# The second norm of a hybrid decoder block: sums by token quarters, stored and fetched rows turned at another place

## The chip, the cores and the metric

The kernel runs on one core of a Trainium2 chip. The metric is the device time of one execution in microseconds. A profile of one execution gives the span (first to last instruction), each instruction's start and duration, and what each engine waited for. The engines are PE (TensorE, with PEld its weight loads), DVE (VectorE), ACT (ScalarE), POOL (GpSimd) and SP, whose queue starts most transfers.

## The reference, cut to what matters

```python
x = x + gate1[:, None, :] * (merged @ w_out[l])
h2 = modulate(rmsnorm(x, norm2_g[l]), shift2, scale2)
x = x + gate2[:, None, :] * peer(h2, peer_wq[l], peer_subkeys[l], peer_u[l], peer_v[l])
# rmsnorm: x * rsqrt(mean(x*x, -1) + EPS) * g;   modulate: h * (1 + scale) + shift
# peer: q = h2 @ wq, 16 blocks of 128 columns (8 heads, 2 halves); scores of each half with 128
# subkeys; the best 16 of each half, then the best 16 of the sums: 128 experts for a token, each
# a row of peer_u and of peer_v, weighted by softmax(scores) * gelu(u . h2)
```

There are 512 tokens and 1024 channels, all in float32. Ahead of this lie the first norm, the input projection, attention and a short convolution; the change leaves them alone.

## The kernel before, in words

Activations lie transposed: `xT` holds 8 blocks of 128 channels by 512 tokens. A float32 product is made from three products of float32r parts (`hi`, made on ScalarE, and `lo` = value minus `hi`, made on VectorE or GpSimd in `split`), by `mm3`: 3 matmuls for each block of 128 channels, 24 for a whole block of outputs. Instructions are issued by a framework that lays out each engine's queue from the dependencies and its own estimate of times: code order is a priority, and an instruction whose inputs are ready may go ahead of earlier code. `after(ins, mark)` adds a wait by hand. `mark[0]` is the last matmul of the latest `mm3`. Tiles of one tag share a fixed number of buffers; the pools `xp` (`xT`) and `tp` (temporary tiles) are closed after the second norm and their space is used again by `r4` and `rp` (subkeys `sk`, queries `qs`, scores).

The path around the change:

- *Output product* (`out_half`, loop at L540): for each of 8 blocks, 24 matmuls into a bank `py`, then VectorE updates `xT` with the gate (L544). ScalarE squares the block before it and VectorE adds the squares up (`squared`, L219). Beside it `more_ada` computes the modulation columns `mod` 30 to 47, three blocks in each of six rounds (L213).
- *Second norm*: the sum of squares over channels is a product with `ones` in a bank `ss2` (L551 for blocks 0 to 6, L552 for block 7), which gives every partition the sums of all 512 tokens. `rstd` (L239) takes root and reciprocal on 128 x 512. The columns `s2` = (1 + scale) * gain are made by L553 and L554 after it in the code.
- `spill` (L528): 32 transposes of `xT` (each 128 x 128), 8 copies `xn` to SBUF and 8 stores to `x1s` in DRAM, so that the rows of x can be added at the kernel's end. They wait for `end`, the last matmul of the sum.
- *Early query blocks*: for two query blocks (`EARLY`) the weights are split ahead, by VectorE. For each of 8 channel blocks `modulated` makes `f` on VectorE (L229), `fH` on ScalarE (L230), `fL` on VectorE (L231), and the 6 matmuls of both query blocks follow.
- *Rows of the fetched tokens* (L584): the last 160 of the 512 tokens get their experts by fetched rows. ScalarE adds the shift to those columns of `f` (L590 spreads the 32 tokens before `TD` over 96 columns more; L592), TensorE transposes 8 blocks for each of two row tiles, ScalarE copies them to `hN` and `h2N`.
- *Query stage* (`query`, `scores`, L721 to L757): for each of 16 blocks 24 matmuls (blocks 0 and 1 have theirs), a copy `qs`, then the scores of the block before (L738: 4 float32 products, 8 instructions), and the best 16 on VectorE (`level1`, `level2`). GpSimd makes the `lo` parts of these weights. After it the dense expert stage begins (`first`).

Of the kernel before, what the change touches and what calls it, by code (L numbers as in the profile page):

```python
# [89 lines left out]
def body(tc, p):  # L90
# [83 lines left out]

    def split(h, l, f, by=nc.vector):
        nc.scalar.activation(h, f, AF.Copy)  # L176
        by.tensor_sub(l, f, h.bitcast(F32))  # L177

# [4 lines left out]

    def parts(src, by=nc.vector):

        raw = load(src)
        h = hl.tile([P, D], F32R, tag="h", bufs=4, name="hi")
        l = hl.tile([P, D], F32R, tag="l", bufs=4, name="lo")
        split(h, l, raw, by)
        return h, l  # L190

    def weights_of(src, by=nc.vector):

        h, l = parts(src.rearrange("p a b -> p (a b)"), by)
        return (lambda k: h[:, k * P:(k + 1) * P]), (lambda k: l[:, k * P:(k + 1) * P])
# [20 lines left out]
    def tmp(name):  # L216
        return tp.tile([P, T], F32, name=name, **T2)
# [16 lines left out]
    def square(ps, b, i, n, w=None):  # L234
        q = tmp("sq")
        nc.scalar.activation(q, b, AF.Square)
        nc.tensor.matmul(ps, ones if w is None else w, q, start=(i == 0), stop=(i == n - 1))

    def rstd(ps, n):  # L239
# [287 lines left out]

    def spill(half, when):  # L528
        for c in range(NCH):
            ps = bank("xt")  # L530
            for i in range(4):
                after(nc.tensor.transpose(ps[:, i * P:(i + 1) * P], xT[:, 4 * half + i, c * P:(c + 1) * P], ident),
                      when)
            xn = rt.tile([P, 512], F32, name="xn", **R2)
            nc.scalar.activation(xn, ps, AF.Copy)
            nc.sync.dma_start(x1s[c][:, half * 512:(half + 1) * 512], xn)

    ss2 = bank("ss2")
    sq = None
    for b in range(DC):  # L540
        if b >= HEAD:
            out_half(b, 0)
        out_half(b, 1)
        nc.vector.scalar_tensor_tensor(xT[:, b, :], py.pop(b), mod[:, 16 + b:17 + b], xT[:, b, :],  # L544
                                       op0=OP.mult, op1=OP.add)
        if 0 < b < DC - 1:
            sq = squared(xT[:, b - 1, :], sq)
        if b < 6:
            more_ada(3)
    sq = squared(xT[:, 6, :], sq)  # L550
    nc.tensor.matmul(ss2, ones, sq, start=True, stop=False)  # L551
    end = nc.tensor.matmul(ss2, ones, squared(xT[:, 7, :]), start=False, stop=True)  # L552
    nc.vector.tensor_add(mod[:, 24:48], mod[:, 24:48], ab[:, 24:48])  # L553
    nc.vector.scalar_tensor_tensor(s2, mod[:, 32:40], 1.0, S("n2g"), op0=OP.add, op1=OP.mult)  # L554
    a1_s.close()
# [18 lines left out]
    fL = hx.tile([P, DC, T], F32R, name="fL")  # L574
    r2 = rstd(ss2, D)
    spill(0, end)
    spill(1, end)
    early = [(weights_of(p["wq"][b]), bank("pq")) for b in range(EARLY)]
    fs = []
    for k in range(DC):  # L580
        fs.append(modulated(fH[:, k, :], fL[:, k, :], xT[:, k, :], r2, s2[:, k:k + 1], mod[:, 24 + k:25 + k]))
        for w, o in early:
            mm3(o, w, lambda k: fH[:, k, :], lambda k: fL[:, k, :], [k])
    for r, (dst, cs) in enumerate(((hN, slice(TD - P, TD)), (h2N, slice(TD, T)))):  # L584
        pg = [bank("pg0"), bank("pg1")]
        for k in range(DC):
            b = mod[:, 24 + k:25 + k]
            f = fs[k]
            if r == 0:
                nc.scalar.activation(f[:, TD - P:TU].rearrange("p (q t) -> p q t", t=HT),  # L590
                                     f[:, None, TU:TD].to_broadcast([P, P // HT - 1, HT]), AF.Identity, bias=b)
                nc.scalar.activation(f[:, TU:T], f[:, TU:T], AF.Identity, bias=b)  # L592
            nc.tensor.transpose(pg[k // 4][:, (k % 4) * P:(k % 4 + 1) * P], f[:, cs], ident)
        for k in range(2):
            nc.scalar.activation(dst[:, k * 512:(k + 1) * 512], pg[k], AF.Copy)
    xp_s.close()
# [121 lines left out]
    def tmp(name):  # L718
        return rp.tile([P, T], F32, tag="t2", name=name, bufs=4)

    def query(hp):  # L721
        sk = rp.tile([P, P], F32, tag="sk", name="sk", bufs=3)
        if hp < EARLY:
            ps = early[hp][1]
        else:
            w = weights_of(p["wq"][hp], nc.gpsimd)
            ps = bank("pq")
            mm3(ps, w, lambda k: fH[:, k, :], lambda k: fL[:, k, :])
        nc.sync.dma_start(sk, p["sk"][hp])
        qs = tmp("qs")  # L730
        nc.scalar.activation(qs, ps, AF.Copy)
        return qs, sk
# [15 lines left out]
    for hp in range(16):  # L748
        so_far = mark[0]
        now = query(hp)  # L750
        if last:
            scores(hp - 1, *last)
            if 2 <= hp < 2 + DC:
                for d, x in ((h2H, fH), (h2L, fL)):
                    after(nc.scalar.activation(d[:, hp - 2, :], x[:, hp - 2, 0:TU].bitcast(F32), AF.Copy), so_far)
        last = now
    scores(15, *last)  # L757
# [374 lines left out]
```

## Time and profile before

| what | value |
|---|---|
| device time, median of 3 executions | 1435.29 us (1432.73 to 1438.98) |
| profiled execution | 1440.74 us, span 1438.9 us |
| busy: PE, PEld | 1395.2 us (97%), 1223.1 us (85%) |
| busy: DVE, ACT, POOL | 1228.5 us (85%), 615.9 us (43%), 468.0 us (33%) |
| mean granted TensorE clock | 0.989 of full |

An engine's share of busy time is an average over stages. A matmul's record lasts from its start to a modelled end, and the next one starts before that; the pace is read from two starts. The bracket behind a row of a timeline is the idle time ahead of it and the instruction that ended it. A row of a timeline can hold several like instructions in a row (x32); its duration is then that of all.

### The profile page before, as it was taken

The page shows a single profiled execution, that of the slowest core. Times are in us where ns is not written, and L with a number is a line of the kernel's source. Part 1 is how long each engine was busy: PE and PEld are TensorE (multiplying, and loading weights), DVE is VectorE, ACT ScalarE, POOL GpSimd, SP SyncE. Part 2 cuts the span into 40 slices and gives each one's busy share as a digit, 9 for nine tenths or more (in the row PEclk, how much of TensorE's full clock was granted, in tenths as well). Part 3 has the DMA queues.
Part 4 walks back from the last instruction along what each step waited for, and adds up shares of the span by engine and source line. Part 5 has one row for each costly group of instructions (what it writes and reads, how often), then busy time and mean ns, then how long its engine had stood idle before and what let it go on. Part 6 is the DMA issues. An engine that isn't in the chain of part 4 may idle for free.

```text
span 1438.9 us, 21241 instructions
## 1 busy us (share of the span) xinstructions
PE 1395.2 (97%) x7696; PEld 1223.1 (85%) x7696; DVE 1228.5 (85%) x2245; ACT 615.9 (43%) x1041; POOL 468.0 (33%) x314
## 2 busy tenths in 40 slices
PE   6999998999999999999999999999999999999998
PEld 4676766888999999989888888889999998889897
DVE  6778978689989999998778898888789889898954
ACT  4524644543735555553433343333343324333431
POOL 0000001343332330043034444546545546655300
PEclk9899999999999999999999999999999999999999
DMA  8545536222497997799999999999999999999843
GB/s 283 192 160 189 191 108 229 87 86 93 127 348 268 389 363 255 251 364 394 350 346 379 391 390 384 401 362 368 351 367 396 382 364 335 381 344 389 310 144 132
DMA packets 134377, 418.81 MB, mean 291 GB/s; under 512 B 12800, under 2 KB 39552, under 8 KB 132736
## 3 DMA queue, kind: packets, MB, share of 16 engines
q1 hardware_dynamic: 92800, 266.45, 51.4%
q0 software_dynamic: 41472, 151.01, 27.5%
q8 instruction: 60, 0.98, 0.3%
q14 instruction: 45, 0.37, 0.1%
HBM read 375.77 MB, written 41.62 MB: 290 GB/s over the span
## 4 chain that ended last, share of the span: by engine, by line
PE 40%; DMA 8%; DVE 5%; issue 5%; POOL 2%; ACT 0%; DVEq 0%; POOLq 0%; ACTq 0%
PE o L998 8%; PE o L997 8%; PE o L996 8%; PE pa L202 5%; PE pa L200 5%; PE pa L201 5%; DMA row<-in_uR,eG 4%; DMA row<-in_vL,eG 3%; POOL row L776 2%; DVE lo L177 1%; DVE junk L784 1%; DMA G<-Gd 1%; DVE ga L912 1%; DVE wwl L177 0%; DVE B L946 0%
## 5 line engine op out<-in xcount | busy, mean ns | idle before, releaser
L176 ACT ACTIVATE hi<-raw 128x1024 fp32r<-128x1024 f32 x298 | 312.5, 1053 | 300.8 <-PE pa L201 92.3
L177 DVE TENSOR_TENSOR lo<-raw,hi 128x1024 fp32r<-128x1024 f32 x276 | 336.2, 1220 | 42.0 <-ACT hi L176 36.5
L200 PE MATMUL pa<-h2H,hi 128*128 128x352 f32 x1024 | 332.9, 325 | 3.1 <-ACT sp L620 3.0
L202 PE MATMUL pa<-h2H,lo 128*128 128x352 f32 x1024 | 331.9, 324 | 3.1 <-DVE lo L177 3.1
L201 PE MATMUL pa<-h2L,hi 128*128 128x352 f32 x1024 | 329.9, 322 | 0.0
L997 PE MATMUL o<-lo,wwh 128*128 128x512 f32 x768 | 299.6, 390 | 1.8 <-DVE lo L177 1.6
L996 PE MATMUL o<-hi,wwh 128*128 128x512 f32 x768 | 299.6, 390 | 0.0
L998 PE MATMUL o<-hi,wwl 128*128 128x512 f32 x768 | 299.0, 389 | 0.2 <-DVE wwl L177 0.2
L776 POOL DMA_INDIRECT row<-in_uR,eG x128 | 190.0, 1484 | 321.0 <-PE o L998 176.9
L776 POOL DMA_INDIRECT row<-in_vL,eG x128 | 177.4, 1386 | 137.9 <-PE o L998 65.3
L784 DVE SCALAR_TENSOR_TENSOR junk<-row,h2N 128x1024 bf16<-128x1024 f32 x128 | 154.2, 1223 | 58.2 <-DMA row<-in_uR,eG 58.0
L202 PEld LDWEIGHTS pa<-h2H,lo 128*128 128x128 f32 x1024 | 194.0, 189 | 5.5 <-DVE lo L177 5.4
L200 PEld LDWEIGHTS pa<-h2H,hi 128*128 128x128 f32 x1024 | 192.8, 188 | 6.0 <-ACT sp L620 3.3
L201 PEld LDWEIGHTS pa<-h2L,hi 128*128 128x128 f32 x1024 | 193.0, 189 | 2.2
L912 DVE SCALAR_TENSOR_TENSOR ga<-row,av,ga 128x1024 f32<-128x1024 f32 x127 | 163.0, 1284 | 28.3 <-DMA row<-in_vL,eG 27.2
L997 PEld LDWEIGHTS o<-lo,wwh 128*128 128x128 f32 x768 | 144.2, 188 | 31.8 <-DVE lo L177 3.7
L998 PEld LDWEIGHTS o<-hi,wwl 128*128 128x128 f32 x768 | 144.2, 188 | 30.7 <-DVE wwl L177 0.6
L996 PEld LDWEIGHTS o<-hi,wwh 128*128 128x128 f32 x768 | 144.2, 188 | 28.0 <-issue 0.2
L177 POOL TENSOR_TENSOR lo<-raw,hi 128x1024 fp32r<-128x1024 f32 x22 | 53.4, 2429 | 322.7 <-ACT hi L176 322.7
L176 ACT ACTIVATE wwh<-w 128x768 fp32r<-128x768 f32 x64 | 54.0, 844 | 162.6 <-DVE w L979 124.3
L978 ACT ACTIVATE w<-G 128x32 f32<-128x32 f32 x128 | 22.3, 221 | 198.2 <-DVE wwl L177 187.9
L776 POOL DMA_INDIRECT row<-in_uR,eH x32 | 47.0, 1470 | 105.2 <-DVE junk L784 88.5
(266 smaller groups left out, 1912.6 us busy)
## 6 DMA issues: line engine op xcount, KB each, us to landing
raw<-in_uL SPq DMA_DIRECT2D x128, 512.0 KB, 6.3
raw<-in_vL SPq DMA_DIRECT2D x128, 512.0 KB, 6.7
Gd<-st SPq DMA_DIRECT2D x12, 2048.0 KB, 10.0
G<-Gd SPq DMA_DIRECT2D x16, 1536.0 KB, 12.5
ada<-in_ada SPq DMA_DIRECT2D x32, 512.0 KB, 4.4
Ad<-sp SPq DMA_DIRECT2D x34, 352.0 KB, 6.4
sp<-Ad SPq DMA_DIRECT2D x34, 352.0 KB, 6.8
raw<-in_w_in SPq DMA_DIRECT2D x18, 512.0 KB, 5.1
```

Source lines behind the costliest of these rows:

```text
L176: nc.scalar.activation(h, f, AF.Copy)
L177: by.tensor_sub(l, f, h.bitcast(F32))
L200: nc.tensor.matmul(ps, wh(k), rh(k), start=(k == k0), stop=False)
L201: nc.tensor.matmul(ps, wh(k), rl(k), start=False, stop=False)
L202: mark[0] = nc.tensor.matmul(ps, wl(k), rh(k), start=False, stop=(k == k1))
L776: d = nc.gpsimd.indirect_dma_start(out=t, out_offset=None, in_=tab, in_offset=bass.IndirectOffsetOnAxis(ap=e, axis=0))
L784: return nc.vector.scalar_tensor_tensor(junk, t, 1.0, h, op0=OP.mult, op1=OP.mult, accum_out=a)
L912: nc.vector.scalar_tensor_tensor(ga, t, av[:, k:k + 1], ga, op0=OP.mult, op1=OP.add)
L978: nc.scalar.activation(wv[:, i, nu:], g[:, i, nu:], AF.Copy)
L996: nc.tensor.matmul(o, wh[:, cs], vh[:, hs], start=(j == 0), stop=False)
L997: nc.tensor.matmul(o, wh[:, cs], vl[:, hs], start=False, stop=False)
L998: last = nc.tensor.matmul(o, wl[:, cs], vh[:, hs], start=False, stop=(j == NJ - 1))
```

## The change

- The modulation columns 24 to 39 and `s2` are finished ahead of the output loop in the code; only columns 40 to 47 stay behind it.
- The `lo` part of early query block 1 waits for the update of `xT` block 6 (`x6`). GpSimd's `lo` part of query block 2 waits for `end`, that of block 3 for `begun`, the last matmul of the early query blocks.
- The sums of squares are made by `grouped`: the tokens of each quarter (128) are summed into 32 partitions of their own, so root and reciprocal run on 128 x 128 (`grouped_root`). `spread` then brings them back to 128 x 512 by four products with one column of the identity, into a PSUM bank, which `modulated` reads in place of an SBUF tile.
- 8 of the 32 transposes of x go behind the last output matmul, ahead of the sums; their 2 copies and stores wait for `end`. The other 24 transposes, 6 copies and stores wait for `begun`. The copies `xn` now use the pool of temporary tiles.
- The 16 activations that prepared the fetched tokens' columns are removed. In query blocks 5, 7, 9 and 11 GpSimd makes these columns as `fH` + `fL` (two additions in each, `f2`), and in blocks 13 and 14 TensorE transposes them and ScalarE copies them.

```diff
@@
-    def split(h, l, f, by=nc.vector):
+    def split(h, l, f, by=nc.vector, when=None):
         nc.scalar.activation(h, f, AF.Copy)
-        by.tensor_sub(l, f, h.bitcast(F32))
+        after(by.tensor_sub(l, f, h.bitcast(F32)), when)
...
+    def grouped(ps, q, first, last):
+
+        for c in range(NCH):
+            end = nc.tensor.matmul(ps[32 * c:32 * c + 32, 0:P], ones[:, 0:32], q[:, c * P:(c + 1) * P], start=first,
+                                   stop=last)
+        return end
+
+    def grouped_root(ps, n):
+        r = cp.tile([P, P], F32, tag="r", name="r", bufs=1)
+        nc.scalar.activation(r, ps[:, 0:P], AF.Sqrt, scale=1.0 / n, bias=eps)
+        nc.vector.reciprocal(r, r)
+        return r
+
+    def spread(r):
+
+        ps = psa.tile([P, 512], F32, tag="a", name="rr")
+        for c in range(NCH):
+            nc.tensor.matmul(ps[:, c * P:(c + 1) * P], ident[:, 32 * c:32 * c + 1].to_broadcast([P, P]), r,
+                             start=True, stop=True)
+        return ps
@@
-    def spill(half, when):
-        for c in range(NCH):
+    def turned(half, when, cs):
+
+        out = []
+        for c in cs:
             ps = bank("xt")
             for i in range(4):
                 after(nc.tensor.transpose(ps[:, i * P:(i + 1) * P], xT[:, 4 * half + i, c * P:(c + 1) * P], ident),
                       when)
-            xn = rt.tile([P, 512], F32, name="xn", **R2)
-            nc.scalar.activation(xn, ps, AF.Copy)
+            out.append((half, c, ps))
+        return out
+
+    def stored(blocks, when):
+        for half, c, ps in blocks:
+            xn = tmp("xn")
+            after(nc.scalar.activation(xn, ps, AF.Copy), when)
             nc.sync.dma_start(x1s[c][:, half * 512:(half + 1) * 512], xn)
 
+    nc.vector.tensor_add(mod[:, 24:40], mod[:, 24:40], ab[:, 24:40])
+    nc.vector.scalar_tensor_tensor(s2, mod[:, 32:40], 1.0, S("n2g"), op0=OP.add, op1=OP.mult)
...
+        if b == DC - 2:
+            x6 = x
...
+    some = turned(0, mark[0], range(2))
     sq = squared(xT[:, 6, :], sq)
-    nc.tensor.matmul(ss2, ones, sq, start=True, stop=False)
-    end = nc.tensor.matmul(ss2, ones, squared(xT[:, 7, :]), start=False, stop=True)
-    nc.vector.tensor_add(mod[:, 24:48], mod[:, 24:48], ab[:, 24:48])
-    nc.vector.scalar_tensor_tensor(s2, mod[:, 32:40], 1.0, S("n2g"), op0=OP.add, op1=OP.mult)
+    grouped(ss2, sq, True, False)
+    end = grouped(ss2, squared(xT[:, 7, :]), False, True)
+    nc.vector.tensor_add(mod[:, 40:48], mod[:, 40:48], ab[:, 40:48])
@@
-    r2 = rstd(ss2, D)
-    spill(0, end)
-    spill(1, end)
-    early = [(weights_of(p["wq"][b]), bank("pq")) for b in range(EARLY)]
-    fs = []
+    r2 = spread(grouped_root(ss2, D))
+    stored(some, end)
+    early = [(weights_of(p["wq"][b], when=x6 if b else None), bank("pq")) for b in range(EARLY)]
     for k in range(DC):
-        fs.append(modulated(fH[:, k, :], fL[:, k, :], xT[:, k, :], r2, s2[:, k:k + 1], mod[:, 24 + k:25 + k]))
+        modulated(fH[:, k, :], fL[:, k, :], xT[:, k, :], r2, s2[:, k:k + 1], mod[:, 24 + k:25 + k])
...
+    begun = mark[0]
+    for half, cs in ((0, range(2, NCH)), (1, range(NCH))):
+        stored(turned(half, begun, cs), begun)
@@
+    f2 = hx.tile([P, DC, 2 * P], F32, name="f2")
+
+    def rows_turned(r):
+
+        pg = [bank("pg0"), bank("pg1")]
+        for k in range(DC):
+            nc.tensor.transpose(pg[k // 4][:, (k % 4) * P:(k % 4 + 1) * P], f2[:, k, r * P:(r + 1) * P], ident)
+        for k in range(2):
+            nc.scalar.activation((hN, h2N)[r][:, k * 512:(k + 1) * 512], pg[k], AF.Copy)
...
-            w = weights_of(p["wq"][hp], nc.gpsimd)
+            w = weights_of(p["wq"][hp], nc.gpsimd, {2: end, 3: begun}.get(hp))
...
+            if hp in (5, 7, 9, 11):
+                k = slice(hp - 5, hp - 3)
+                sq = [P, 2, P // HT, HT]
+                after(nc.gpsimd.tensor_add(f2[:, k, 0:P].rearrange("p k (q t) -> p k q t", t=HT),
+                                           fH[:, k, None, TU:TD].bitcast(F32).to_broadcast(sq),
+                                           fL[:, k, None, TU:TD].bitcast(F32).to_broadcast(sq)), so_far)
+                nc.gpsimd.tensor_add(f2[:, k, P:], fH[:, k, TD:].bitcast(F32), fL[:, k, TD:].bitcast(F32))
+            if hp in (13, 14):
+                rows_turned(hp - 13)
```

## Rows read from the trace of the kernel before

**Rows 1.** Stage windows: length; PE, PEld, DVE, ACT, POOL busy; clock, DMA, GB/s

```profile
300.00:352.00 52.00, 52.00 (x265) 44.00 (x263) 46.99 (x304) 19.07 (x37) 19.25 (x8) 1.00 0.28 91
352.00:400.00 48.00, 45.76 (x288) 44.99 (x287) 46.26 (x135) 32.22 (x38) 17.64 (x9) 1.00 0.45 142
...
500.00:700.00 200.00, 192.37 (x1527) 185.32 (x1526) 192.70 (x439) 103.84 (x177) 37.94 (x25) 0.99 0.87 326
```

**Rows 2.** TensorE in order of time: start, duration, instruction, [idle before, releaser]

```profile
236.39 0.39 PE L202 MATMUL py<-mH,lo 128*128 128x512 f32 x1
238.23 1.13 PE L551 MATMUL ss<-sq,ones 128*128 128x512 f32 x2 [1.46 <-DVE sq L223]
239.56 1.12 PE L552 MATMUL ss<-sq,ones 128*128 128x512 f32 x2 [0.20 <-ACT sq L221]
240.52 3.66 PE L532 MATMUL xt<-cst,xT 128*128 128x128 f32 x32
247.16 1.22 PE L200 MATMUL pq<-fH,hi 128*128 128x512 f32 x2 [2.99 <-ACT fH L230]
...
259.38 0.39 PE L201 MATMUL pq<-fL,hi 128*128 128x512 f32 x1
259.61 0.40 PE L202 MATMUL pq<-fH,lo 128*128 128x512 f32 x1
...
261.59 1.06 PE L738 MATMUL psc<-sk,qs 128*128 128x128 f32 x8
262.40 0.48 PE L200 MATMUL pq<-fH,hi 128*128 128x512 f32 x1
```

**Rows 3.** Engines by stretch as in 1, around the clock's fall

```profile
244.20:247.10 2.90, 0.00 (x0) 0.00 (x0) 2.67 (x4) 1.80 (x4) 0.00 (x0) 1.00 0.67 256
247.10:249.00 1.90, 1.84 (x4) 1.40 (x5) 1.86 (x3) 1.90 (x5) 0.00 (x0) 0.52 0.81 312
```

**Rows 4.** VectorE in order of time, around the second norm

```profile
232.63 2.37 DVE L554 SCALAR_TENSOR_TENSOR s<-mod,sm 128x8 f32<-128x8 f32 x1
...
236.05 0.74 DVE L544 SCALAR_TENSOR_TENSOR xT<-py,mod,xT 128x512 f32<-128x512 f32 x1
237.48 0.69 DVE L223 TENSOR_TENSOR sq<-sq 128x512 f32<-128x512 f32 x1 [0.70 <-ACT sq L221]
238.09 0.75 DVE L544 SCALAR_TENSOR_TENSOR xT<-py,mod,xT 128x512 f32<-128x512 f32 x1
...
241.44 3.35 DVE L242 RECIPROCAL rstd<-rstd 128x512 f32<-128x512 f32 x1 [2.45 <-ACT rstd L241]
...
253.88 0.75 DVE L229 SCALAR_TENSOR_TENSOR f<-xT,s,rstd 128x512 f32<-128x512 f32 x1
```

**Rows 5.** ScalarE in order of time, around the second norm

```profile
238.87 0.63 ACT L221 ACTIVATE sq<-xT 128x512 f32<-128x512 f32 x1 [0.47 <-DVE xT L544]
240.72 0.69 ACT L241 ACTIVATE rstd<-ss,eps 128x512 f32<-128x512 f32 x1 [1.22 <-PE ss L552]
...
245.29 1.21 ACT L535 ACTIVATE xn<-xt 128x512 f32<-128x512 f32 x2 [2.42 <-DMA x1s<-xn]
246.39 0.71 ACT L230 ACTIVATE fH<-f,mod 128x512 fp32r<-128x512 f32 x1
```

**Rows 6.** GpSimd in order of time, before the second norm

```profile
232.34 2.62 POOL L177 TENSOR_TENSOR lo<-raw,hi 128x1024 fp32r<-128x1024 f32 x1 [231.89 <-ACT hi L176]
```

**Rows 7.** Groups by line and shape: busy, mean ns, idle before

```profile
L741 ACT ACTIVATE scg<-psc 128x128 f32<-128x128 f32 x16 | 4.5, 282 | 0.0
...
L403 DVE RECIPROCAL den<-den 128x8 f32<-128x8 f32 x4 | 0.8, 198 | 0.0
```

**Rows 8.** SP's DMA issues in order of time

```profile
254.69 1.28 SPq L729 DMA_DIRECT2D sk<-in_sk  x3
```

**Rows 9.** DMA issues by tile: size, median us to landing

```profile
sk<-in_sk SPq DMA_DIRECT2D x16, 64.0 KB, 1.7
```

More of the change, by code (lines that the diff above doesn't have):

```diff
@@ L182, in load, with parts @@
         return raw
-    def parts(src, by=nc.vector):
+    def parts(src, by=nc.vector, when=None):
         raw = load(src)
@@ L188, in parts, with weights_of @@
         l = hl.tile([P, D], F32R, tag="l", bufs=4, name="lo")
-        split(h, l, raw, by)
+        split(h, l, raw, by, when)
         return h, l
-    def weights_of(src, by=nc.vector):
-        h, l = parts(src.rearrange("p a b -> p (a b)"), by)
+    def weights_of(src, by=nc.vector, when=None):
+        h, l = parts(src.rearrange("p a b -> p (a b)"), by, when)
         return (lambda k: h[:, k * P:(k + 1) * P]), (lambda k: l[:, k * P:(k + 1) * P])
@@ L543, in body @@
         out_half(b, 1)
-        nc.vector.scalar_tensor_tensor(xT[:, b, :], py.pop(b), mod[:, 16 + b:17 + b], xT[:, b, :],
-                                       op0=OP.mult, op1=OP.add)
+        x = nc.vector.scalar_tensor_tensor(xT[:, b, :], py.pop(b), mod[:, 16 + b:17 + b], xT[:, b, :],
+                                           op0=OP.mult, op1=OP.add)
+        if b == DC - 2:
+            x6 = x
         if 0 < b < DC - 1:
@@ L574, in body @@
     fL = hx.tile([P, DC, T], F32R, name="fL")
-    r2 = rstd(ss2, D)
-    spill(0, end)
-    spill(1, end)
-    early = [(weights_of(p["wq"][b]), bank("pq")) for b in range(EARLY)]
-    fs = []
+    r2 = spread(grouped_root(ss2, D))
+    stored(some, end)
+    early = [(weights_of(p["wq"][b], when=x6 if b else None), bank("pq")) for b in range(EARLY)]
     for k in range(DC):
-        fs.append(modulated(fH[:, k, :], fL[:, k, :], xT[:, k, :], r2, s2[:, k:k + 1], mod[:, 24 + k:25 + k]))
+        modulated(fH[:, k, :], fL[:, k, :], xT[:, k, :], r2, s2[:, k:k + 1], mod[:, 24 + k:25 + k])
         for w, o in early:
             mm3(o, w, lambda k: fH[:, k, :], lambda k: fL[:, k, :], [k])
[L584 to L595, printed above, removed]
+    begun = mark[0]
+    for half, cs in ((0, range(2, NCH)), (1, range(NCH))):
+        stored(turned(half, begun, cs), begun)
     xp_s.close()
```

## The prediction, made before the result was known

> **What bounds the kernel now.** I read the stage table first. From the first query product to the end TensorE sets the pace: in the query stage it is busy in every microsecond of 300 to 352, VectorE in 46.99 of 52 [rows 1]. A microsecond that TensorE loses before 262 us is therefore a microsecond of the end, and so is each matmul added later. Next I read TensorE in order of time around the second norm [rows 2]. The last output product starts at 236.39 and lasts 0.39, so it ends at 236.78; the third query block starts at 262.40. Everything the change touches lies in these 25.6 us. TensorE idles 1.46 before the first sum of squares, about 0.2 before the second, then runs 32 transposes from 240.52, idles 2.99, and starts the query products at 247.16. [...] One such matmul follows another after 0.23 (259.38 to 259.61), so 48 want 10.9; the stretch from 247.16 to 259.84, where the next work started, was 12.7. The slow clock cost 1.7.
>
> Last I read the chain behind those gaps on VectorE, ScalarE and GpSimd [rows 4 to 6]. x of block 6 was ready to be made once its product was done (231.4, 24 matmuls before 236.78), but started at 236.05: the 8-column s2 in front of it took 2.37, for it lies inside a GpSimd lo part running from 232.34 to 234.96, and then came a lo part of VectorE's own. Block 7 then stood behind block 6's square and its addition and started at 238.09, 1.25 after the product it needs. From there: square 0.63, sum 1.12 to 240.68, root 0.69, reciprocal 3.35 on 512 columns, first scaled block at about 244.8, and its fH at 246.39 instead of about 245.6, because two copies of transposed rows, themselves held 2.42 by a store, stood ahead on ScalarE.
>
> **The change, along that path.** All times are those of the profiled execution, 1440.74 us with a span of 1438.9; the median of the runs shown is 1435.29, and I take the same difference off it.
>
> The scale s2 moves ahead, the lo part of query block 1 waits for x of block 6, and GpSimd's lo parts for blocks 2 and 3 wait for the end of the sum and of the early products. Then block 6 is done by about 232.2 and its square and addition by about 234, and block 7 starts 0.06 after its product: 236.84 to 237.59, square to 238.25. What queues behind the held parts can bear it: on VectorE only the addition and block 7; on GpSimd only later lo parts. Block 2's lo runs 2.6 from about 239.5 and is wanted near 258; block 3's runs from about 254.6 to 257.2 and is wanted 6.4 later than that of block 2.
>
> TensorE fills the wait with 8 of the 32 transposes at 0.11 each (32 took 3.66), to 237.65. The sums by quarters are new. The nearest rows are the score products, 8 instructions on 128 columns: 1.06 from start to end, 0.81 until the next work starts. Bounds: 0.27 if the four strips of 32 outputs run side by side, 1.12 if they cost what the full sum did. I take the scores' price, since shape and count are theirs: the first group to 238.46, the second to 239.5. That is 1.2 ahead of 240.68.
>
> Root on 128 columns: 0.28, as the 128-column copy from PSUM [rows 7], to 239.85. Reciprocal: 8 columns took 0.20 [rows 7] and 512 took 3.35, so 128 want 0.95, to 240.8. Spreading the quarters back over 512 columns is four more such products, 1.06, to 241.9. Then f 0.75, now read with 1/rms in PSUM (block updates, which also read PSUM, take 0.74 to 0.75 too [rows 4]), fH 0.72 with only two row copies near it, both done in the reciprocal's shadow: TensorE starts at 243.5, which is **3.6 ahead** of 247.16.
>
> Does the clock fall again? Idle 1.46 at 236.8 was not followed by a lower clock, idle 2.99 at 244.2 was [rows 2, 3]. The new gaps are about 1.35 (239.5 to 240.85) and 1.6 (241.9 to 243.5), nearest to the first. I take no fall: 48 matmuls in 10.9, to 254.5, 5.3 ahead of 259.84. VectorE keeps up, with 16 operations on eight blocks at some 0.65 each (14 of them from 244.8 to the last f at 253.88).
>
> [...]
>
> Now what was hidden comes due. The other 24 transposes stood in a wait before; now they follow the early products on a busy TensorE: 2.6, to 257.1. The 16 transposes of the fetched tokens' rows go from here to query blocks 13 and 14, where they cost the same 1.75. The scores of block 0 take 0.81, and block 2 starts at 257.9, 4.5 ahead of 262.40. With 1.75 paid later, **2.7 us** remain.
>
> Moved things that I cost at nothing: ScalarE loses 16 small activations; it is busy 19.07 of 52 in the query stage [rows 1]. The stores of x move from 242 to about 256 on SP's queue, 0.33 an issue, and are read only at the kernel's end. GpSimd gets eight additions of 256 elements; 1024 took 2.62 [rows 6], so 0.6 each, bounds 0.6 and 2.6, in blocks of 6.4 where it has one lo part of 2.6. Without that cover they would delay the lo part of a later query block. VectorE's 5 idle microseconds in 52 hide what it waits for them.
>
> **Rivals.** *The clock falls all the same.* Light work from 236.8 to 243.5 with 3 us of idling speaks for it, the short gaps against it. It costs up to 1.7: gain 1.0, 1434.3 us.
>
> *The scores wait.* The subkeys' load started at 254.69, right after the last f read xT (253.88 and 0.74) [rows 4, 8], so it seems to lie in xT's space. Now xT is read by transposes until 257.3; a load takes 1.7 to land [rows 9], so block 0's scores could start at 259.1, not 257.1. Six row copies of about 0.6 ahead of the query copy on ScalarE end near there too. If TensorE's queue has the scores ahead of block 2, 2.0 are lost: gain 0.7, 1434.6 us; with a fallen clock 1.0 slower, 1436.3. Against it: the queues are laid out by readiness, as s2, late in the code, ahead of block 6 shows.
>
> *GpSimd's additions make VectorE the bound* (the other side). The place is query blocks 5 to 12, where VectorE's candidate sums read two SBUF tensors, as s2 does. If each addition took 2.6 and held VectorE that long, 8 would give 21 against some 5 of slack: 16 late, less the 2.7, so 13 slower, 1448. It decides (7.2 slower) from 1.9 per addition on. Against it: lo parts of 2.6 in every block already lie beside a VectorE with time to spare.
>
> [...]
>
> *The rest of the program is laid out anew.* An edit here can shift orders later on. TensorE idles 2.2 from 352 to 400 and 7.6 from 500 to 700 [rows 1]; if that vanished the gain would be 12.5, 1423; if it doubled, 7.1 slower, 1442 or a little over.
>
> *The change doesn't do what it says*: block 6 stays late by another neighbour. Then 1.25 of the lead is lost, gain 1.4, 1433.9.
>
> **Numbers.** Forecast, gain 2.7: 1432.6 us, chance 0.42. Clock falls 0.22, scores wait 0.16, laid out anew 0.13, additions on GpSimd 0.04, block 6 late 0.03. The most the region could give is its idle 4.65 and the clock's 1.7, less 1.06 for spreading: 5.3, 1430.0. The worst of the small cases is 1436.3. Three runs lay from 1432.73 to 1438.98, so I widen by 1 below, and by 2 above for a milder new layout: 1429.0 to 1438.5. About 0.5%, 7.2 us, is what a measurement of this kernel tells from no change: beyond it lie, of the new layout's 0.13, 0.04 on the fast side and 0.04 on the slow one, and 0.02 of the GpSimd case. So faster 0.04, same 0.90, slower 0.06.
>
> **What would show it.** Block 6's update near 231.5 and block 7's within 0.1 of its product; a reciprocal near 0.95; the first early product near 243.5; granted clock near 1.00 in the 4 us behind it; 24 transposes back to back after the early products with no wait before the next scores; candidate sums still at 0.3. I'd be wrong if the early products start after 245, if TensorE waits for subkeys or for rows' banks near 257, or if the lead of 4.5 at block 2 does not stand at the first dense block less 1.75.

## The result and the profile after

The changed kernel takes 1446.26 us (median of 6 executions, 1442.51 to 1450.59) beside 1434.57 (6 executions, 1432.73 to 1438.98) of the kernel before: a ratio of 1.0076, 95% interval 1.0057 to 1.0096. It is 11.7 us slower where 2.7 less had been forecast, and outside the range.

| profiled execution | before | after |
|---|---|---|
| time, span | 1440.74, 1438.9 us | 1447.71, 1445.9 us |
| busy PE, DVE | 1395.2, 1228.5 us | 1392.2, 1223.5 us |
| mean granted clock | 0.989 | 0.989 |
| end of the last output product | 236.78 | 231.91 |
| first dense product | 353.7 | 359.5 |
| between these two, the *stretch* | 116.9 | 127.6 |

Nothing of this can be seen in shares of busy time. The end of the last output product varies between executions with nothing edited ahead of it (227.85 in a second profile of the kernel before), so times are best read from that point. The stretch from there to the first dense product has grown by 10.7. The rest has not: from the first dense product to the end of the span it is 1438.9 - 353.7 = 1085.2 before and 1445.9 - 359.5 = 1086.4 after (1083.3 to 1091.6 over all profiles below, 1089.2 in the second of the kernel before). Nearly all the loss lies in the stretch.

TensorE of the changed kernel in order of time, in the form of [rows 2]:

```profile
231.52 0.39 PE L202 MATMUL py<-mH,lo 128*128 128x512 f32 x1
231.75 1.04 PE L555 MATMUL xt<-cst,xT 128*128 128x128 f32 x8
232.72 0.43 PE L242 MATMUL ss<-sq,ones 128*32 128x128 f32 x8
233.42 0.43 PE L242 MATMUL ss<-sq,ones 128*32 128x128 f32 x8 [0.28 <-ACT sq L221]
235.32 1.16 PE L256 MATMUL rr<-r,cst 128*128 128x128 f32 x8 [1.47 <-DVE r L249]
238.07 1.22 PE L200 MATMUL pq<-fH,hi 128*128 128x512 f32 x2 [1.60 <-ACT fH L230]
...
252.23 2.84 PE L555 MATMUL xt<-cst,xT 128*128 128x128 f32 x24
263.27 2.04 PE L769 MATMUL psc<-sk,qs 128*128 128x128 f32 x8 [8.20 <-DMA sk<-in_sk]
264.97 0.77 PE L200 MATMUL pq<-fH,hi 128*128 128x512 f32 x1
...
272.04 1.05 PE L769 MATMUL psc<-sk,qs 128*128 128x128 f32 x8
```

The early products start 238.07 - 231.91 = 6.2 behind the last output product; before it was 247.16 - 236.78 = 10.4 [rows 2] (10.2 in the second profile of the kernel before). So the first half of the change gives 4.2. Then three things go wrong. The 48 early products last 14.16, to 252.23. The 24 transposes end at 255.07, and the scores of block 0 wait 8.20 for the subkeys. These scores and block 2 behind them are slow: 1.70 to the next start instead of 0.81, and 7.07 for the 24 products, which took 5.59 in the kernel before (262.40 to the next scores at 267.99).

The stages, as in [rows 1, 3], show the clock and the DMA:

```profile
236.50:238.00 1.50, 0.00 (x0) 0.00 (x0) 1.49 (x3) 0.70 (x2) 0.00 (x0) 0.81 0.51 184
238.00:244.00 6.00, 5.92 (x13) 4.24 (x14) 6.00 (x10) 3.37 (x6) 1.89 (x2) 0.50 0.19 73
...
254.80:263.20 8.40, 0.28 (x3) 0.04 (x1) 0.00 (x0) 3.43 (x7) 4.69 (x3) 0.69 0.90 277
259.00:266.50 7.50, 3.23 (x12) 2.97 (x13) 0.62 (x4) 0.66 (x2) 1.64 (x1) 0.50 0.96 325
...
300.00:352.00 52.00, 52.00 (x270) 44.18 (x269) 46.14 (x297) 19.93 (x41) 20.58 (x11) 1.00 0.29 91
```

The clock is 0.50 in the first six microseconds of the early products, and 0.50 again around the scores (259.00 to 266.50). While TensorE waits, the DMA engines are 0.90 busy. The query stage (last line) is as full as before.

What TensorE waits for is one line of the table of waits (engine, what, releaser: total, times, longest). SP's queue in order of time then shows why the load came so late:

```profile
PE psc L769 <- DMA sk<-in_sk: 8.2, 1, 8.2
```

```profile
234.79 0.81 SPq L564 DMA_DIRECT2D x1s<-xn  x2
236.38 18.83 SPq L181 DMA_DIRECT2D raw<-in_wq  x2
255.31 4.04 SPq L564 DMA_DIRECT2D x1s<-xn  x6
259.45 1.76 SPq L760 DMA_DIRECT2D sk<-in_sk  x3
```

The durations of the single issues of stores (ns: least, median, most):

```profile
L564 SPq DMA_DIRECT2D x1s<-xn x8: 326/413/972, 234.8 to 258.8; - x8
```

The subkeys stand behind two weight loads, the second of which holds the queue until 255.21, and behind six stores, which take 4.04. The row copies are done by 256.31 (the rows of ScalarE below), so it isn't they that make these stores slow: an issue itself lasts up to 0.97. Why is not shown. The issue of the subkeys at 259.45 is 4.4 later than the end of the last transpose, which frees the space. The scores start 3.82 after it, when the first load has landed, behind 1.5 MB of stores and half a megabyte of weights; the median landing before was 1.7 [rows 9].

VectorE, ScalarE and GpSimd, as in [rows 4 to 6]:

```profile
227.42 0.74 DVE L574 SCALAR_TENSOR_TENSOR xT<-py,mod,xT 128x512 f32<-128x512 f32 x1
...
231.95 0.75 DVE L574 SCALAR_TENSOR_TENSOR xT<-py,mod,xT 128x512 f32<-128x512 f32 x1 [1.93 <-PE py L202]
...
234.31 0.95 DVE L249 RECIPROCAL r<-r 128x128 f32<-128x128 f32 x1 [1.46 <-ACT r L248]
236.51 2.07 DVE L229 SCALAR_TENSOR_TENSOR f<-xT,s,rr 128x512 f32<-128x512 f32 x3 [1.25 <-PE rr L256]
```

```profile
233.91 0.37 ACT L248 ACTIVATE r<-ss,eps 128x128 f32<-128x128 f32 x1 [0.55 <-PE ss L242]
...
253.31 3.00 ACT L563 ACTIVATE xn<-xt 128x512 f32<-128x512 f32 x6
256.16 1.12 ACT L762 ACTIVATE qs<-pq 128x512 f32<-128x512 f32 x2
```

```profile
234.02 2.34 POOL L177 TENSOR_TENSOR lo<-raw,hi 128x1024 fp32r<-128x1024 f32 x1 [233.57 <-PE ss L242]
239.98 1.17 POOL L793 TENSOR_TENSOR f<-fH,fL 128x256 f32<-128x256 f32 x1 [3.63 <-DVE fL L231]
...
247.48 0.73 POOL L793 TENSOR_TENSOR f<-fH,fL 128x256 f32<-128x256 f32 x1 [1.65 <-DVE fL L231]
252.48 4.67 POOL L177 TENSOR_TENSOR lo<-raw,hi 128x1024 fp32r<-128x1024 f32 x2 [4.27 <-PE pq L202]
```

Block 7 starts 0.04 after its product, and the reciprocal is 0.95. The last line of GpSimd is the one that holds SP's queue: the first of these two lo parts ends near 254.8, half of 4.67 behind its start, and the second weight load, which had waited for a buffer of raw weights, is issued.

### The profile page after: what moved, and what is told of

Its sections match the earlier page's. It is cut to its first block, busy times and chain, and to the rows that moved or that the text cites. A ratio compares the mean times of both kernels' runs of the same rounds, so it can differ in the third digit from the quotient of the medians.

```text
span 1445.9 us, 21281 instructions
## 1 busy us (share of the span) xinstructions
PE 1392.2 (96%) x7716; PEld 1221.5 (84%) x7716; DVE 1223.5 (85%) x2246; ACT 611.8 (42%) x1025; POOL 459.4 (32%) x322
## 4 chain that ended last, share of the span: by engine, by line
PE 39%; issue 6%; DMA 5%; DVE 5%; POOL 3%; ACT 0%; POOLq 0%; SPq 0%; DVEq 0%
PE o L1037 7%; PE o L1038 7%; PE o L1036 7%; PE pa L200 5%; PE pa L202 5%; PE pa L201 5%; DMA row<-in_uR,eG 4%; POOL row L816 3%; DVE lo L177 1%; DVE junk L824 1%; DMA Ad<-sp 1%; DVE B L986 1%; DMA sp<-Ad 1%; DVE wwl L177 0%; DVE w L1019 0%
## 5 line engine op out<-in xcount | busy, mean ns | idle before, releaser
L816 POOL DMA_INDIRECT row<-in_uR,eG x128 | 183.7, 1435 | 331.2 <-PE o L1038 185.5
L816 POOL DMA_INDIRECT row<-in_vL,eG x128 | 168.5, 1316 | 144.1 <-PE o L1038 75.1
```

The lines of the kernel that those rows point to most:

```text
L816: d = nc.gpsimd.indirect_dma_start(out=t, out_offset=None, in_=tab, in_offset=bass.IndirectOffsetOnAxis(ap=e, axis=0))
```

## The experiments

Two theories stood at the start. *Scores* (S in the forecasts): most of the loss is block 0's scores waiting for a load that lies in `xT`'s space and queues behind stores and weights. *Holds* (H): GpSimd's held lo parts are the cause, since they hold the weight load that blocks SP. Beside both, the slow early products were to be explained. The stretch is measured in the one profiled execution of each, as in the table above. A ratio is to the kernel before as it ran beside that version, so ratios are compared and not times; their intervals reach 0.0016 to 0.0028 to either side, 2 to 4 us.

**The subkeys in a space of their own.** They need not wait for `xT`, and their load goes ahead.

```diff
-        sk = rp.tile([P, P], F32, tag="sk", name="sk", bufs=3)
+        sk = hx.tile([P, P], F32, tag="sk", name="sk", bufs=3)
```

> The changed kernel, but the subkeys' tiles lie beside fH and fL instead of in the space that xT gives back, so their first three loads stand ahead of the stores of x in SP's queue; TensorE's order is the same. Theory S (the 8.2 us wait of block 0's scores is the subkeys' load, which must wait for xT's last transposes and for six stores ahead of it in SP's queue): the wait is gone, TensorE goes from the last transposes to the scores without a gap, and the clock does not fall there, so about 8.2 of wait, 1 of slow scores and 1.4 of slow products of block 2 come back: 1435 to 1437 us. Rival H (the held lo part of block 3 blocks SP's queue by the weight load behind it): that load and the stores are where they were, so something else in the queue is still late and at most 2 us come back: 1444 or more.

Measured: 1436.70 us, ratio to before 1.0014 (0.9996 to 1.0033), stretch 118.9. This one line moves 9 of the 11.7 us. Its TensorE, then SP's queue:

```profile
237.29 1.22 PE L200 MATMUL pq<-fH,hi 128*128 128x512 f32 x2 [1.60 <-ACT fH L230]
251.43 2.84 PE L555 MATMUL xt<-cst,xT 128*128 128x128 f32 x24
256.05 1.16 PE L769 MATMUL psc<-sk,qs 128*128 128x128 f32 x8 [1.77 <-ACT qs L762]
```

```profile
231.16 1.28 SPq L760 DMA_DIRECT2D sk<-in_sk  x3
```

The wait of 8.20 is gone; what ends last now is the query copy on ScalarE, behind six row copies. The scores then take 0.91 to the next start (256.05 to 256.96), with the clock at 1.00 from 256 to 262. The early products still take 251.43 - 237.29 = 14.1. So the two losses are separate.

**No holds on GpSimd's lo parts.**

```diff
-            w = weights_of(p["wq"][hp], nc.gpsimd, {2: end, 3: begun}.get(hp))
+            w = weights_of(p["wq"][hp], nc.gpsimd, None)
```

> The changed kernel without the two holds of GpSimd's lo parts of blocks 2 and 3; SP's weight loads move ahead of the stores as a result, TensorE's order is the same. Rival H: the queue is free when the first row copy is made, the subkeys are issued near 254 in the times of the changed kernel and most of the 8.2 us wait goes: 1437 to 1440 us. Theory S: the subkeys stay behind xT's transposes and six stores; the first store leaves about 1.4 earlier (253.9 instead of 255.3) and half a megabyte less is under way, so 1 to 2.5 of the wait go: 1443 to 1445.5 us.

Measured: 1447.18 us, 1.0098 (1.0072 to 1.0124), stretch 127.9, wait 8.53. The theory of the holds falls; but the 1 to 2.5 that theory S had forecast did not go either. SP's queue and GpSimd show why:

```profile
253.10 0.33 SPq L181 DMA_DIRECT2D raw<-in_wq  x1
253.48 4.13 SPq L564 DMA_DIRECT2D x1s<-xn  x6
257.71 1.77 SPq L760 DMA_DIRECT2D sk<-in_sk  x3
```

```profile
250.71 2.36 POOL L177 TENSOR_TENSOR lo<-raw,hi 128x1024 fp32r<-128x1024 f32 x1 [4.61 <-ACT hi L176]
```

The weight load still waits for a lo part that ends at 253.07, just when the last transpose ends (253.08). That part waits for its hi part on ScalarE, which waited for the early products, whose weights hold its buffer. The hold that was taken away had another one behind it.

**The six late stores on ScalarE's queue.**

```diff
-            nc.sync.dma_start(x1s[c][:, half * 512:(half + 1) * 512], xn)
+            (nc.sync if when is end else nc.scalar).dma_start(x1s[c][:, half * 512:(half + 1) * 512], xn)
```

> The changed kernel with the six late stores of x issued from ScalarE's queue instead of SP's; the subkeys still lie in xT's space and still wait for its last transposes. It parts theory S in two. If the place behind six issues makes the wait, the subkeys are issued at about 255.3 instead of 259.45 (behind the weight load that waits for the held lo part), land in 2 to 4 us, and the wait falls from 8.2 to 2.5 to 5: 1439 to 1442 us. If it is the transfers (1.6 MB of stores at some 300 GB/s are 5 us), the subkeys land about as late as before, at 261 or later, and the wait is 6 or more: 1444 or more.

Measured: 1445.30 us, 1.0068 (1.0044 to 1.0091), stretch 127.9. It doesn't test what it was made for, since the blocking moved. SP's queue, its stores gone, took a third weight load ahead of the subkeys (issued at 258.49), and on ScalarE the query copy stood behind the issue of the stores:

```profile
257.75 6.02 ACTq L564 DMA_DIRECT2D x1s<-xn  x2
263.82 1.09 ACT L762 ACTIVATE qs<-pq 128x512 f32<-128x512 f32 x2 [5.61 <-DMA raw<-in_wq]
```

A copy that needs nothing from any transfer starts 5.61 late, since the issue of two stores stands ahead of it in its engine's queue and lasts 6.02.

**The six late stores left out** (the kernel's end adds rows of another input in their place, so part of the result is left out).

```diff
-            nc.sync.dma_start(x1s[c][:, half * 512:(half + 1) * 512], xn)
+            if when is end:
+                nc.sync.dma_start(x1s[c][:, half * 512:(half + 1) * 512], xn)
...
-        nc.sync.dma_start(x1, x1s[c])
+        nc.sync.dma_start(x1, p["uR"][c * P:(c + 1) * P, :])
```

> The changed kernel with the six late stores of x left out (the rows added at the kernel's end are taken from other data in their place, so that part of the result is left out); the subkeys still lie in xT's space and wait for its last transposes, and TensorE's order is the same. Theory S, in the form that the stores make most of the wait: what is left is xT's release, the weight load behind the held lo part and a landing of 1.7 us, so the wait of block 0's scores falls from 8.2 to 2 to 2.6, the clock hardly falls behind it: 1437.5 to 1440 us. Rival, that xT's space alone makes the wait: it stays at 6 or more, 1443 us or more.

Measured: 1442.60 us, 1.0062 (1.0034 to 1.0089), wait 6.11, stretch 125.1. Without stores the wait is 2.1 shorter, not gone, so theory S (2 to 2.6) missed, and the number fits its rival (6 or more). But again a third weight load stood ahead of the subkeys (issued at 255.83), and the scores started 3.6 after their issue, so the space alone isn't shown to make the wait. The next version takes that weight load away too.

**No holds and no late stores** (the same part of the result left out).

> The changed kernel without GpSimd's two holds and without the six late stores of x (the rows added at the kernel's end are taken from other data, so that part of the result is left out). Each alone left most of the wait (8 and 6.1 us). Theory S: each blocker stands in front of the same queue, and with one gone the other is next; with both gone the first subkeys leave right behind one weight load, some 0.5 after xT's last transposes, and land in 2 to 3.5: a wait of 2.3 to 4 us, 1438 to 1441 us. Rival: xT's release and the landing make the wait by themselves: 6 or more, 1442 us or more.

Measured: wait 3.78, stretch 121.2, and 1445.47 us, 1.006 (1.0033 to 1.0087). The wait is as the theory of the queue has it: with both blockers gone the subkeys are issued 0.45 after the last transpose. The time isn't (1438 to 1441 had been forecast): in its profile 1445.7 - 354.1 = 1091.6 lie behind the stretch, the longest of all, though each of the two edits alone had 1083.3 and 1083.5 there. Whether that is chance stays open.

**The first three subkey loads on ScalarE's queue**, past everything on SP's.

```diff
-        nc.sync.dma_start(sk, p["sk"][hp])
+        (nc.scalar if hp < 3 else nc.sync).dma_start(sk, p["sk"][hp])
```

> The changed kernel with the first three loads of subkeys issued from ScalarE's queue, where they stand behind the six row copies but behind no store and no weight load; they still lie in xT's space. TensorE's order is the same. Theory S in its present form (xT's release, then SP's queue in order, then a landing beside the stores): in the times of the changed kernel the first load is issued at about 256.3 instead of 259.45 and lands 2 to 4 later beside the stores, so the wait falls from 8.2 to 3.3 to 5.3: 1439 to 1442.5 us. If the transfers that are under way set the landing, whatever the queue, it lands at 261 or later, the wait is 6 or more, and the time 1443.5 or more.

Measured: 1444.59 us, 1.0059 (1.0032 to 1.0086), stretch 123.9, 3.7 shorter than that of the change, of which 2.4 show in the ratio. The wait of 4.29 lies in its forecast, the time 2 above. TensorE:

```profile
257.96 2.05 PE L769 MATMUL psc<-sk,qs 128*128 128x128 f32 x8 [4.29 <-DMA sk<-in_sk]
```

The load is issued at 253.79, as soon as the space is free, and still lands only for 257.96, beside six stores on SP's queue. So the wait of 8.20 is about half order in the queue (0.24 for the held weight load, 4.1 for the stores) and half landing (3.8). The stores look like the smaller part of that landing: in the two versions without late stores the scores started 3.6 and 3.3 after the issue, beside weight loads alone.

**The transposes moved ahead.** All 32 wait for `end` only: 12 run while the reciprocal is made, 12 behind the spreading; copies and stores go with them.

```diff
     stored(some, end)
+    for half, cs in ((0, range(2, NCH)), (1, range(NCH))):
+        stored(turned(half, end, cs), end)
...
     begun = mark[0]
-    for half, cs in ((0, range(2, NCH)), (1, range(NCH))):
-        stored(turned(half, begun, cs), begun)
```

> The changed kernel with the 24 late transposes, their copies and stores put behind the end of the sum of squares (12 before the spreading products, 12 behind them) instead of behind the early query products. Theory S: xT is free when its last block is scaled, the subkeys arrive in time, the 8.2 us wait goes, and 2.6 us of transposes lie in gaps again; against that the six copies stand ahead of the first fH on ScalarE and cost 1 to 2: 1432 to 1436 us. On the clock: if transposes do not keep it, the early products start slow again as in the changed kernel (about 14 us for 48 matmuls); if they do, about 11, and the time is 3 lower. Rival H: the weight load behind the held lo part still keeps the subkeys to about 255.5, a wait of 3 or more stays: 1439 or more.

Measured: **1433.02 us, 0.9981 (0.9965 to 0.9998)**, stretch 113.6: 14.0 shorter than that of the change. TensorE, then a stage:

```profile
232.25 1.53 PE L555 MATMUL xt<-cst,xT 128*128 128x128 f32 x12
233.79 1.16 PE L256 MATMUL rr<-r,cst 128*128 128x128 f32 x8
234.78 1.47 PE L555 MATMUL xt<-cst,xT 128*128 128x128 f32 x12
237.65 0.73 PE L200 MATMUL pq<-fH,hi 128*128 128x512 f32 x2 [1.40 <-ACT fH L230]
...
250.02 1.16 PE L769 MATMUL psc<-sk,qs 128*128 128x128 f32 x8 [0.77 <-ACT qs L762]
```

```profile
238.00:244.00 6.00, 5.95 (x26) 4.60 (x25) 6.00 (x9) 2.86 (x5) 2.37 (x2) 1.00 0.57 189
```

`xT` is read last by f, so the subkeys are issued at 245.54 and TensorE no longer waits for them (it waits 0.77 for the query copy). And the clock stays at 1.00: the 48 products take 11.4. With transposes in the gaps it was kept.

**Copies held.** The same, with the last three row copies held behind the second, third and fourth fH (`done` is the instruction that makes fH), since eight copies stood ahead of the first.

```diff
...
+    stored(turned(0, end, range(2, NCH)) + turned(1, end, range(1)), end)
+    others = turned(1, end, range(1, NCH))
...
+        if 1 <= k <= 3:
+            stored(others[k - 1:k], done)
```

> The kernel with all transposes of x behind the sum (1433.0 us), with the last three row copies held behind the first fH instead of ahead of it on ScalarE. The first fH should then follow its f at once, 1.0 earlier, and the early products start 1.0 earlier: 1431 to 1433 us, a ratio to the kernel before of 0.996 to 0.999. It is also a second look at the clock in that form: if the 24 transposes in the two gaps keep it, the 48 early products take 11 to 11.7 us again; if the first profile was chance, about 14, and the time is 1434 to 1436 us.

Measured: 1433.56 us, 0.9988 (0.9972 to 1.0004), stretch 114.6. The idle time ahead of the early products fell from 1.40 to 0.29, but 0.22, 0.22 and 0.48 came up between them, where the copies now stand. From the first start to the last end the 48 products last 13.8 (239.03 to 252.82) beside 11.6 (237.65 to 249.25) without the holding, though the clock was 1.00 again; 11 to 11.7 had been forecast. No gain.

**Gaps filled with matmuls**, on top of the first experiment: five matmuls of 512 columns, of no use to the result, after the sums and five after the spreading (`eh` is the hi part of an early query block's weights; the loop stands once for each of the two blocks `b`; `last[0]` is the last spreading product).

```diff
...
+        for i in range(5):
+            after(nc.tensor.matmul(fillb, eh[:, 0:P], eh[:, 0:512], start=(b == i == 0), stop=(b == 1 and i == 4)),
+                  (end, last[0])[b])
```

> The changed kernel with the subkeys beside fH and fL, and ten more matmuls of 512 columns whose result nothing reads: five behind the sum of squares and five behind the spreading products, in the two gaps of TensorE ahead of the early products. If the clock falls there because the gaps hold too little work, it now stays at its upper level, the 48 early products take about 11 us instead of 14.2, and the time is some 3 below that of the kernel with only the subkeys moved: 1432.5 to 1434.5 us. If the clock falls at that place whatever TensorE does, the early products take about 14 again and the time is 1436 to 1438 us.

Measured: 1436.00 us, 1.0009 (0.9987 to 1.0032), stretch 118.2, against 118.9 with the gaps. The stages:

```profile
238.00:244.50 6.50, 6.50 (x31) 5.26 (x30) 3.80 (x6) 2.06 (x3) 3.10 (x3) 1.00 0.00 0
...
249.00:251.00 2.00, 1.89 (x10) 1.79 (x11) 0.00 (x0) 1.69 (x4) 0.85 (x2) 0.65 0.87 281
251.00:253.00 2.00, 2.00 (x6) 1.61 (x5) 1.68 (x12) 0.29 (x1) 1.94 (x1) 0.50 1.06 405
```

The early products run at a clock of 1.00 and take 11.9 instead of 14.1. But after the 24 transposes and the 1.77 of waiting for the query copy the clock falls to 0.65 and 0.50, where it was 1.00 in the first experiment: from these scores to the next it takes 8.1 (249.11 to 257.22) instead of 6.5 there (256.05 to 262.56), and 1.6 is lost again.

**Plain sums**, on top of the transposes moved ahead: the sums by quarters undone, root and reciprocal on 512 columns again.

```diff
-    grouped(ss2, sq, True, False)
-    end = grouped(ss2, squared(xT[:, 7, :]), False, True)
+    nc.tensor.matmul(ss2, ones, sq, start=True, stop=False)
+    end = nc.tensor.matmul(ss2, ones, squared(xT[:, 7, :]), start=False, stop=True)
...
-    r2 = spread(grouped_root(ss2, D))
+    r2 = rstd(ss2, D)
```

> The kernel with all transposes of x behind the sum (1433.0 us), with the sums by quarters undone: one product with ones over 512 columns, root and reciprocal on 512 columns, no spreading, 1/rms from SBUF. From the rows: the sum ends 0.7 later, the root takes 0.35 more, the reciprocal 2.4 more, the spreading products (about 1.1 with their handoff) fall away: the early products start 2.3 to 2.7 later, 1435 to 1436 us. The rival is that the transposes cover the reciprocal anyway and the sums by quarters are worth nothing: 1433 us. If the longer gap lets the clock fall, 1.5 to 3 more: 1437 to 1439 us.

Measured: 1441.01 us, 1.0047 (1.0023 to 1.0072), stretch 120.0, which is above all three forecasts. TensorE, then VectorE:

```profile
241.44 0.79 PE L200 MATMUL pq<-fH,hi 128*128 128x512 f32 x1 [6.23 <-ACT fH L230]
```

```profile
239.88 1.42 DVE L229 SCALAR_TENSOR_TENSOR f<-xT,s,rstd 128x512 f32<-128x512 f32 x2 [3.18 <-DMA x1s<-xn]
```

6.4 more than with the quarters: 4.2 of it is the later start (11.5 behind the last output product instead of 7.3), the rest goes with the clock, which fell over the 6.23 of waiting (0.52 from 241 to 247). But the later start isn't the price of the sums alone: the reciprocal was done at 236.70, and the first f then waited 3.18 for a buffer that a store of x was still reading. So what the quarters are worth by themselves is not shown.

**Late scale, no holds**, on top of the transposes moved ahead: s2 and the lo parts as before the change, the one of early query block 1 too.

```diff
-    nc.vector.tensor_add(mod[:, 24:40], mod[:, 24:40], ab[:, 24:40])
-    nc.vector.scalar_tensor_tensor(s2, mod[:, 32:40], 1.0, S("n2g"), op0=OP.add, op1=OP.mult)
...
-    nc.vector.tensor_add(mod[:, 40:48], mod[:, 40:48], ab[:, 40:48])
+    nc.vector.tensor_add(mod[:, 24:48], mod[:, 24:48], ab[:, 24:48])
+    nc.vector.scalar_tensor_tensor(s2, mod[:, 32:40], 1.0, S("n2g"), op0=OP.add, op1=OP.mult)
...
-    early = [(weights_of(p["wq"][b], when=x6 if b else None), bank("pq")) for b in range(EARLY)]
+    early = [(weights_of(p["wq"][b], when=None), bank("pq")) for b in range(EARLY)]
...
-            w = weights_of(p["wq"][hp], nc.gpsimd, {2: end, 3: begun}.get(hp))
+            w = weights_of(p["wq"][hp], nc.gpsimd, None)
```

> e4_turn_early with the first part of the change (block 6's early scale and held tile) and the holds on GpSimd's lo parts undone. If that part only removes the wait for block 6 where block 6 is late (1.46 us of idle time in the first profile of before, none in the second), it is worth 0 to 1.3 us on the mean: 1433 to 1434.5 us, ratio to before 0.998 to 1.000. Rival: the held lo parts order the weight loads on SP's queue, with no holds a load or the GpSimd's work comes at another time and the kernel is 2 us or more away, on either side.

Measured: 1436.04 us, 1.0011 (0.9993 to 1.0028), stretch 119.0, so 5.4 longer than with both. The rival is nearer. 1.1 of the 5.4 is what the first part of the change had removed: s2 takes 2.37 again, beside a GpSimd lo part (223.40 to 225.84), block 7 starts 1.1 behind its product, and the early products start 8.4 behind the last output product instead of 7.3. The rest goes with a weight load that now lies just ahead of the first store (issued at 231.74 and 232.12; with both, no weight load lay between 228.09 and 237.82): the stores' landing takes a median of 4.6 instead of 2.7, and the second f waits for a buffer that a store still reads. VectorE, then TensorE:

```profile
223.50 2.37 DVE L585 SCALAR_TENSOR_TENSOR s<-mod,sm 128x8 f32<-128x8 f32 x1
...
236.73 1.41 DVE L229 SCALAR_TENSOR_TENSOR f<-xT,s,rr 128x512 f32<-128x512 f32 x2 [2.45 <-DMA x1s<-xn]
```

```profile
236.20 0.73 PE L200 MATMUL pq<-fH,hi 128*128 128x512 f32 x2 [1.39 <-ACT fH L230]
238.85 0.80 PE L201 MATMUL pq<-fL,hi 128*128 128x512 f32 x1 [1.92 <-DVE fL L231]
```

After these two gaps the clock is 0.66 from 236 to 246. Early scale and all the holds were undone together, so which of them keeps the load away stays open.

**The kernel before once more**, for what varies by itself.

> The kernel before, unchanged, for a second profile. In the first one the output products ended at 236.78 us; in the changed kernel and four experiments they ended between 229.8 and 232.7, though nothing ahead of them was edited. If the stages ahead merely vary from one execution to the next, they end near 231 here and the execution is near the median of 1435; if the edits shortened the stages ahead, they end near 236.8 again. The stretch from there to the first dense product should be 117 either way.

Measured: 1436.73 us in one execution, stretch 117.9:

```profile
238.02 1.22 PE L200 MATMUL pq<-fH,hi 128*128 128x512 f32 x2 [4.04 <-ACT fH L230]
```

The gap of 2.99 in [rows 2] is 4.04 here, and the 48 products last 13.8 instead of 12.7. The idle 1.46 ahead of the first sum is absent, and block 7 is on time, for s2 runs ahead of GpSimd's lo part and takes 0.16 instead of 2.37: what the early scale removes isn't in every execution.

## Why the prediction was wrong

From the end of the last output product, block 2 was to start at 257.9 - 236.78 = 21.1; it started at 264.97 - 231.91 = 33.1. The 12.0 between them, by the steps:

| step | predicted | measured | difference |
|---|---|---|---|
| last output product to first early product | 6.7 | 6.2 | -0.6 |
| 48 early products | 10.9 | 14.2 | +3.3 |
| 24 transposes | 2.6 | 2.8 | +0.2 |
| wait for the subkeys | 0 | 8.2 | +8.2 |
| scores of block 0 | 0.8 | 1.7 | +0.9 |

Block 2 itself adds 1.5 (7.07 for 5.59, with the clock at 0.50 up to 266.50). With the 2.7 that had been forecast, 12.0 + 1.5 - 2.7 = 10.8, the growth of the stretch to 0.1.

**What failed first** is the step "moved things that I cost at nothing": "The stores of x move from 242 to about 256 on SP's queue, 0.33 an issue, and are read only at the kernel's end." The stores' readers were looked at, not what queues behind them. The subkeys did: they waited out a weight load and six stores, at 0.67 each rather than 0.33, and then landed in 3.8. The rival *the scores wait for the subkeys* had the place and the mechanism, with the space of `xT` free only after the last transpose, and is shown by two experiments that free the load in different ways, the space of its own and the transposes moved ahead: in both the wait is gone. Its price of 2.0 took a free queue and the median landing of 1.7 [rows 9]; it measured 8.2, and the chance of 0.16 was too low, as was its objection that queues are laid out by readiness. A framework that works from estimates had put the load behind a weight load whose issue waits for GpSimd.

**What failed next** is "I take no fall". After 1.47 and 1.60 of idling the clock fell to 0.50, as it did to 0.52 after 2.99 before [rows 2, 3]; the one idle of 1.46 without a fall, on which the step rested, was a single instance, and the rows don't show why it was spared. The rival had a price of 1.7; it was 3.3. It isn't a fixed price: behind the same two gaps the 48 products took 14.1 to 14.3 in six versions and 12.9 in the one with no holds and no late stores. That the gaps are the cause is shown by the two ways of filling them, 11.4 and 11.9 for the 48 products; with matmuls in them nothing else differs from the first experiment, which took 14.1. Transposes in the gaps were enough in two runs (the transposes moved ahead; the copies held): with 24 of them there the clock was 1.00. In two more (plain sums; late scale, no holds) it fell behind such transposes, to 0.52 and 0.66, but over 6.23 of idling, and over 1.39 and 1.92. In the kernel before the 32 transposes were followed by 2.99 of nothing.

**What held.** Block 7 came as said. Block 6 came 0.8 later than said (4.5 ahead of the end of the last output product for 5.3), behind a lo part of VectorE's own, which cost nothing. The lead of the first half came, 4.2 for 3.6, the difference a sum of 0.43 that had been priced at 0.81 by the scores, so nearer to the lower bound of 0.27. The reciprocal is 0.95 as scaled from the 512 columns; spreading 1.16 for 1.06. The fetched tokens' transposes cost 0.80 in block 13 (343.32 to the next product at 344.12) and 0.79 in block 14, 1.6 for 1.75. GpSimd's additions, priced at 0.6, take 0.73 in the query blocks; four of the eight, which no `after` holds, went ahead into the early products and took 0.73 to 1.84 there, the longer ones beside VectorE's f and fL (the rows of GpSimd above); VectorE is 46.14 of 52 in the query stage, so that rival fell. So did the new layout, as the loss is in the stretch.

With the transposes in the gaps the stretch is 113.6, where 116.9 - 2.7 = 114.2 had been forecast for the change, and the median is 1433.02 for 1432.6. That is luck: up to block 2 this version takes 20.5 for 21.1, but it doesn't pay the 2.6 of transposes that the sum charged, and pays 0.5 more ahead of the early products and 1.5 more from there to the scores, 0.8 of it the wait for the query copy.

## What to carry to other kernels

A transfer that is moved is priced on the queue that it moves to: list what stands behind it there, what that waits for, and how much data lands beside it. When a tile is released later, look for what is loaded into its space; its first reader pays for the release, the queue and the landing together (here 4.4 from the last transpose to the issue, and 3.8 to the landing). Work taken out of a gap of TensorE cost twice here, once where it went (2.8 for the 24 transposes) and once in the clock (3.3 in the early products), so the work that had to be done anyway was best left in the gap (11.4 for the 48 products with the transposes in it, 14.2 without).

## What had not been expected of the hardware

- Four products into 32 partitions each, 128 columns (eight instructions in the trace), take 0.43 together (0.36 to the next start in the version with the transposes moved, 231.89 to 232.25), where the eight instructions of four scores, into 128 partitions, take 1.06 [rows 2].
- A load of 64 KB lands in 1.9 with no store beside it (the version with the transposes moved), 3.1 beside two weight loads (late stores left out) and 4.8 beside stores on another queue and weight loads (stores on ScalarE), the median of the first three loads in the first and the last and of four in the second.
- After 24 transposes and 1.77 of idling the clock fell to 0.65 and 0.50 in the version with the filling matmuls and was 1.00 in the first experiment. What differs between them was not found. Nor did the same gaps cost the same each time (14.1 to 14.3 and 12.9 for 48 products, as above).
